# S5 stage of a two-layer decoder trunk: rows go to chunks without norm, scales are applied to the copies behind

## The chip, the cores and the metric

The kernel runs on one core of a Trainium2 chip. The metric is device time in microseconds of one execution; the time shown is the median of three runs. A profiled execution of the same kernel gives the trace.

## The reference

Two layers on x (256 tokens by 1024 features, float32). Each layer is half a SwiGLU FFN, a mixer, and half a SwiGLU FFN, each with an RMS norm ahead and added to x. The mixer of layer 0 is windowed attention and pooling; that of layer 1 is an S5 state-space layer with GELU and a gated projection:

```
def _rmsnorm(x, g):
    y = xf * lax.rsqrt(jnp.mean(xf * xf, axis=-1, keepdims=True) + EPS)
    return y * g
...
x = x + 0.5 * _swiglu(_rmsnorm(x, ffn_norm[layer, 0]), w_gate, w_up, w_down)
h = _rmsnorm(x, mix_norm[layer])
mixed = _even_mixer(h, ...) if layer % 2 == 0 else _odd_mixer(h, ...)
x = x + mixed
x = x + 0.5 * _swiglu(_rmsnorm(x, ffn_norm[layer, 1]), ...)
...
# _odd_mixer: u = h in 64 groups of 16 channels, 64 complex states a group
bu = einsum('bsgc,gpc->bsgp', u, bb)              # bb from b, a, dt
h_t = lbar * h_(t-1) + bu_t                       # over 256 tokens
y = Re(einsum('bsgp,gcp->bsgc', h, c)) + d_skip * u
z = gelu(y);  val, gate = split(z @ w_glu, 2);  mixed = val * sigmoid(gate)
```

## The kernel before

All float32 weights are split into a high part (an activation on ScalarE, `hi_of`, line 176) and a low part (a subtraction on VectorE into `wl`, line 133), and each product is three matmuls on TensorE, `mm3`. The stages follow one another: FFN f0, the even mixer, FFN f1, FFN f2, the S5 front, the gated projection (units y), FFN f3. An FFN is 11 groups of 256 hidden features; a group needs three units of weights (two of gate and up together, one of down), and a unit is loaded in two raw tiles of 512 KB (line 234).

The program is a list of steps, `S(fn, *units)`. Before each step `pump` splits as many coming units as the ring of four split units has room for, and `fill` issues their loads into four raw buffers. The list `units` is in the order of first use, but `early` puts the S5 units K0, K1, y0, y4, W0, W1 ahead at the place of the first of them. A scheduler turns the list into a queue for each engine by order of emission; a `prio(CHAIN)` moves an instruction ahead. `keep("name", i)` remembers an instruction and `behind("name")` says that what is issued under it stands behind that instruction in the order of its queue. `strict` holds TensorE to the order of emission. `hold` and `release` stop and resume the splits.

The S5 matrices are built from the parameters by the generator `s5_build`, which runs beside the steps of f1 and f2: at each paced step, of which there are five a group, `run_gens` gives it 0.8 of a turn, a turn being the code up to its next `yield`; what is left is let out at `drain`, ahead of group 8 of f2. Its first turn, in f1, issues the loads of a, log_dt, b and c (lines 741 to 756) on SP's queue. Its results go to DRAM, the matrices `dW` (input) and `dK` (the direct part within a chunk of eight tokens), and come back as the units W0, W1, K0 and K1. K takes a slot of the ring with no split, and has two loads of 1 MB (line 271). A gain vector, `gvec`, is loaded for every norm (line 320), behind the last weight load emitted.

In the tail of f2 (`tail`) the two halves c of the features of each tile t of 128 tokens are finished in turn: `x_update`, then its squares, then `norm(t, "m1", True)` (line 350 and on: squares on ScalarE with a running sum, rstd by a power on GpSimd at line 364, product with gvec on VectorE at line 142). `s5_put` (line 1010) sends the normed rows in 16 transfers of 64 KB into `V`, where a partition holds a chunk of eight tokens. `warm` has TensorE run matmuls on zeros meanwhile. Then, for each quarter k of the groups: `s5_front` (lines 1032 and 1034) copies the quarter from V into the order that the transposes want, `s5_uT` transposes, `s5_win` multiplies with the input matrices, `s5_direct` with K, `s5_scan` transposes back and runs the scan on VectorE. After the first win the order is the list `ORDER`, "f1 u1 hold d0 s0 f2 u2 w1 s1 f3 u3 ...", f for front, u for uT, w for win, d for direct, s for scan.

Of the kernel before, what the change touches and what calls it, by code (L numbers as in the profile page):

```python
# [23 lines left out]
EPS = 1e-6  # L24
# [4 lines left out]
WARM = 32  # L29
# [22 lines left out]

C_ID = 0
# [5 lines left out]
C_N = C_IF + 8  # L59


def shape_constants():
# [17 lines left out]
    c[:, C_IF:C_IF + 8] = np.asarray(INV_FREQ, np.float32)  # L80
    return c
# [23 lines left out]
def trunk_kernel(ctx: ExitStack, tc: tile.TileContext, I, out):  # L105
# [115 lines left out]
    def emit_dma(i):  # L221
# [3 lines left out]
        if kind == "W":  # L225
            r = wraw.tile([128, 1024], F32, tag="raw", name="rawW")
            c0 = (i % 2) * 1024
            with behind("put"):
                SP.dma_start(out=r, in_=s5["dW"][2 + units[i // 2][1]][:, c0:c0 + 1024])
            raws[i] = r  # L230
            return
# [18 lines left out]
    late = None  # L250

    def split_late():

        nonlocal late
        late = []

    def split_now(n, *names):
        nonlocal late
        with behind(*names):
            for _ in range(min(n, len(late))):  # L260
                keep("late", tt(*late.pop(0)))
        if not late:
            late = None

    def emit_split(i):
        if units[i][0] == "K":
            n = units[i][1]
            tl = [wsp.tile([128, 2048], F32, tag=tg, name=f"K{n}") for tg in ("wh", "wl")]
            def load(q):
                c0 = 4096 * n + 2048 * q  # L270
                SP.dma_start(out=tl[q], in_=s5["dK"][:, c0:c0 + 2048])
            load(0)
            if n:
                s5["more"] = lambda: load(1)
            else:
                load(1)
# [10 lines left out]
        for p in range(2):  # L287
# [3 lines left out]
            with behind(*(["split"] if i + p else ["norm"])):  # L291
                hi = hi_of(h[s], r)
                if late is None:
                    keep("splits", hi, tt(l[s], r, h[s].bitcast(F32), ALU.subtract))
                else:
                    keep("latehi", hi)
                    late.append((l[s], r, h[s].bitcast(F32), ALU.subtract))
# [437 lines left out]
    def s5_build():  # L735
        b = tc.alloc_tile_pool(name="s5b", bufs=1)

        def new(nm, shape, dt=F32):
            return b.tile([128] + list(shape), dt, name="b_" + nm)
        araw = b.tile([32, 2, 128], F32, name="b_araw")  # L740
        SP.dma_start(out=araw[:, 0], in_=I["s5_a_re"][0].rearrange("(j g) p -> j (g p)", g=2))
        SP.dma_start(out=araw[:, 1], in_=I["s5_a_im"][0].rearrange("(j g) p -> j (g p)", g=2))
        ld = new("ld", [64])
        SP.dma_start(out=ld, in_=I["s5_log_dt"][0].partition_broadcast(128))
        br = new("br", [2, 32, 16])
        SP.dma_start(out=br[:, 0], in_=I["s5_b_re"][0].rearrange("(j g) p c -> (g p) j c", g=2))
        SP.dma_start(out=br[:, 1], in_=I["s5_b_im"][0].rearrange("(j g) p c -> (g p) j c", g=2))
        E = s5["E"]
        cr = E[:, 1].rearrange("p a b n -> p (a b n)")[:, 0:1024].rearrange("p (r q g n) -> p r q g n", r=2, q=4, g=2)
        for r, nm in enumerate(("s5_c_re", "s5_c_im")):  # L750
            for q in range(4):
                src = I[nm][0][16 * q:16 * (q + 1)].rearrange("(j g) c p -> g j c p", g=2)
                for g in range(2):
                    SP.dma_start(out=cr[:, r, q, g], in_=src[g])
# [110 lines left out]

        X = s5["X"]
# [13 lines left out]
        st = new("st", [1024])  # L880
# [51 lines left out]
        db = cbd.rearrange("p r j g c -> p (r j g c)")[:, 0:1024]  # L932
        SP.dma_start(out=db[96:128], in_=I["s5_d"][0].partition_broadcast(32))
        Kf = K0.rearrange("p h j q n -> p (h j) (q n)")
        dv = db[96:128].rearrange("p (n c) -> p n c", c=16)
        tt(dv, dv, im[96:128].unsqueeze(1).to_broadcast([32, 64, 16]), ALU.mult)
# [49 lines left out]
    def s5_run_open():  # L986
# [4 lines left out]
        s5["G"] = p.tile([128, 2, 8, 4, 33], F32, name="G")  # L991
        R = s5["R"].rearrange("p k (q n) -> p (k q) n", n=33)
# [5 lines left out]
    def s5_put(t):  # L998

        V = s5["V"]  # L1000
        jobs = [(t, h, j) for h in range(2) for j in range(4)]
        if t == 0:
            s5["put"], jobs = jobs[-2:], jobs[:-2]
        else:
            jobs[4:4] = s5.pop("put")
        for t, h, j in jobs:
# [538 lines left out]
```

## Time and profile before

| | us |
|---|---|
| median of three runs | 956.82 |
| the three runs | 955.5 to 957.04 |
| the profiled execution | 954.66 |
| its span, first to last instruction | 952.9 |
| TensorE busy in the span | 928.8 |
| VectorE busy | 644.7 |
| ScalarE busy | 435.7 |

Times in the trace are microseconds from the start of the span. PE is TensorE's matmuls and PEld its weight loads, which overlap them; DVE is VectorE, ACT ScalarE, POOL GpSimd, and SPq the queue of SyncE, which issues most transfers; its duration is that of the issue. `out<-in` names the tiles. Of an instruction the bracket shows how long its engine was idle before it, and what ended the wait.

### The profile page before, as it was taken

Reading aid. Unit: us, or ns where it says so; the run is one execution under the profiler, and the core shown is the slowest. Engines: PE = TensorE matmul, PEld = TensorE weight load, DVE = VectorE, ACT = ScalarE, POOL = GpSimd, SP = SyncE. Lnnn points to the kernel's source line nnn. Section 1 sums busy time; section 2 is a strip of 40 time slices with the busy share of each in tenths; the row PEclk is TensorE's granted clock in tenths of the full one; section 3 lists DMA queues with packets and bytes.
Section 4 is the critical chain, followed back from the end, with each engine's and each line's share of the span. In section 5 each row is a group of like instructions: output and inputs, shape, how many; then the busy total and the mean of one; then the engine's idle time right before and its main releaser. Section 6 shows DMA issues by size and latency. Waiting matters only on the chain.

```text
span 952.9 us, 13635 instructions
## 1 busy us (share of the span) xinstructions
PE 928.8 (97%) x5208; PEld 772.4 (81%) x5208; DVE 644.7 (68%) x1097; ACT 435.7 (46%) x643; POOL 58.8 (6%) x105
## 2 busy tenths in 40 slices
PE   8999999999998999999999999999979999999998
PEld 5788888889986888888788888888659988888886
DVE  5646654488876799998675899953596575554452
ACT  6544444455635444445454444443535364444440
POOL 0000000013020000004100250000000000000000
PEclk9999999999999999999999999999999999999999
DMA  8867656644477664569756695567656457556641
GB/s 248 266 192 228 196 180 197 191 141 157 139 166 223 195 196 135 179 211 337 256 171 192 160 285 189 177 200 265 208 214 204 151 160 233 182 178 198 196 135 45
DMA packets 146033, 185.23 MB, mean 194 GB/s; under 512 B 18896, under 2 KB 128400, under 8 KB 145200
## 3 DMA queue, kind: packets, MB, share of 16 engines
q1 hardware_dynamic: 142720, 175.97, 58.9%
q0 software_dynamic: 3248, 8.39, 3.3%
q8 instruction: 41, 0.67, 0.3%
q14 instruction: 24, 0.20, 0.1%
HBM read 173.85 MB, written 9.44 MB: 192 GB/s over the span
## 4 chain that ended last, share of the span: by engine, by line
PE 72%; DVE 15%; DMA 5%; issue 3%; ACT 3%; POOL 1%; SPq 1%; POOLq 0%; ACTq 0%; DVEq 0%
PE wk L95 44%; PE acc L95 21%; PE sk L95 6%; DVE wl L133 4%; DMA raw<-in_ffn_w_up_dram 3%; DVE X L133 1%; ACT wh L176 1%; DMA raw<-in_ffn_w_down_dram 1%; POOL r L604 1%; DVE b_q L133 1%; DVE h L142 1%; DVE b_t L133 1%; DMA gvec<-in_ffn_norm_dram 1%; DVE hTl L133 1%; DVE rot L133 1%
## 5 line engine op out<-in xcount | busy, mean ns | idle before, releaser
L133 DVE TENSOR_TENSOR wl<-raw,wh 128x1024 fp32r<-128x1024 f32 x304 | 363.9, 1220 | 161.8 <-ACT wh L176 160.9
L176 ACT ACTIVATE wh<-raw 128x1024 fp32r<-128x1024 f32 x304 | 312.0, 1055 | 257.8 <-PE wk L95 98.8
L95 PE MATMUL wk<-wh,hTh 128*128 128x512 f32 (+1 forms) x868 | 230.8, 376 | 1.3 <-DVE pr L133 0.9
L95 PE MATMUL wk<-wh,hTl 128*128 128x512 f32 (+1 forms) x868 | 224.9, 370 | 1.2 <-DVE hTl L133 1.2
L95 PE MATMUL wk<-wl,hTh 128*128 128x512 f32 (+1 forms) x868 | 225.7, 370 | 0.0
L95 PEld LDWEIGHTS wk<-wh,hTl 128*128 128x128 f32 x868 | 158.5, 189 | 29.0 <-DVE hTl L133 1.6
L95 PEld LDWEIGHTS wk<-wl,hTh 128*128 128x128 f32 x868 | 158.9, 190 | 28.0 <-DVE wl L133 0.2
L95 PEld LDWEIGHTS wk<-wh,hTh 128*128 128x128 f32 x868 | 154.8, 189 | 26.5 <-DVE pr L133 1.2
L95 PE MATMUL acc<-wh,hh 128*128 128x512 f32 x352 | 141.2, 401 | 0.0
L95 PE MATMUL acc<-wh,hl 128*128 128x512 f32 x352 | 137.9, 392 | 0.5 <-DVE hl L133 0.5
L95 PE MATMUL acc<-wl,hh 128*128 128x512 f32 x352 | 137.5, 391 | 0.0
L420 ACT ACTIVATE sg<-wk 128x256 f32<-128x256 f32 x88 | 33.2, 382 | 114.8 <-PE wk L95 112.4
L133 DVE TENSOR_TENSOR pr<-sg,wk 128x256 f32<-128x256 f32 x88 | 36.6, 416 | 65.9 <-ACT sg L420 65.7
L95 PEld LDWEIGHTS acc<-wh,hl 128*128 128x128 f32 x352 | 66.0, 188 | 15.0 <-DVE hl L133 1.2
L95 PEld LDWEIGHTS acc<-wl,hh 128*128 128x128 f32 x352 | 66.3, 188 | 12.4
L95 PEld LDWEIGHTS acc<-wh,hh 128*128 128x128 f32 x352 | 66.1, 188 | 12.4 <-issue 0.2
L176 ACT ACTIVATE hh<-sk 128x256 fp32r<-128x256 f32 x88 | 32.8, 373 | 29.0 <-PE sk L95 28.9
L133 DVE TENSOR_TENSOR hl<-sk,hh 128x256 fp32r<-128x256 f32 x88 | 36.6, 418 | 5.4 <-ACT hh L176 5.3
L95 PEld LDWEIGHTS sk<-ident,pr 128*128 128x128 f32 x176 | 24.3, 140 | 12.2 <-DVE pr L133 0.6
L95 PE MATMUL sk<-ident,pr 128*128 128x128 f32 x176 | 33.6, 272 | 0.3 <-DVE pr L133 0.2
L364 POOL TENSOR_TENSOR rstd<-ss,mhalf 128x1 f32<-128x1 f32 x12 | 7.5, 623 | 389.3 <-DVE ss L142 389.3
L142 DVE SCALAR_TENSOR_TENSOR h<-x,rstd,gvec 128x512 f32<-128x512 f32 (+1 forms) x25 | 17.2, 728 | 14.9 <-DMA gvec<-in_ffn_norm_dram 7.9
(277 smaller groups left out, 679.5 us busy)
## 6 DMA issues: line engine op xcount, KB each, us to landing
raw<-in_ffn_w_gate_dram SPq DMA_DIRECT2D x88, 512.0 KB
raw<-in_ffn_w_up_dram SPq DMA_DIRECT2D x88, 512.0 KB
raw<-in_ffn_w_down_dram SPq DMA_DIRECT2D x88, 512.0 KB
raw<-in_ev_w_in_dram SPq DMA_DIRECT2D x16, 512.0 KB
raw<-in_s_w_glu_dram SPq DMA_DIRECT2D x16, 512.0 KB
raw<-in_ev_w_out_dram SPq DMA_DIRECT2D x8, 512.0 KB
K<-dK SPq DMA_DIRECT2D x4, 1024.0 KB
dK<-E POOLq DMA_DIRECT2D x36, 64.0 KB, 4.8
```

The source lines that it names most:

```text
L95: i = f(*a, **k)
L133: return DVE.tensor_tensor(out=o, in0=a, in1=b, op=op)
L142: return DVE.scalar_tensor_tensor(out=o, in0=a, scalar=s, in1=b, op0=op0, op1=op1)
L176: return ACT.activation(out=o, in_=i, func=AF.Copy)
L364: POOL.tensor_tensor(out=rstd, in0=ss[:, 2:3], in1=mhalf, op=ALU.pow)
L420: ACT.activation(out=sg, in_=ps[:, 0], func=AF.Silu)
L604: POOL.tensor_tensor(out=r8, in0=s8, in1=mhalf.to_broadcast([128, 8]), op=ALU.pow)
```

## The change

- The puts go out from x itself, right behind each `x_update` of a half c: two for each tile after c=0, six after c=1. The norm of the S5 input and its gain load are gone. The gain is multiplied into the B matrices (`gb`) and into D (`dg`) in the build.
- rstd of each row is brought into V's order, where a partition is a chunk and a column one of its eight tokens, by `s5_scale`: m8 × rstd, a small matmul with the 0/1 matrix `sel`, and a copy into `rV`. `s5_front` multiplies with it: quarters 0 and 1 by two multiplies on VectorE each, quarters 2 and 3 by eight activations on ScalarE each, with a column of rV as scale.
- `early` becomes y0, y4, W0, W1, K0, K1. K's loads are issued behind the last put emitted; the late splits (`split_late`, `split_now`, `s5["more"]`) are gone, and W's loads no longer stand behind the puts.
- The build's loads stand behind the last weight load emitted and are spread over turns, so that the generator has 12 turns more, one of them for the multiplies with gb.
- The warm matmuls are 10 + 10 instead of 32, with the small matmul of the scale between.

```diff
-WARM = 32
+WARM = 20
...
+    tok = np.arange(128)[:, None]
+    c[:, C_SE:C_SE + 64] = tok // 8 == np.arange(64)[None, :] % 16
+    c[:, C_M8:C_M8 + 8] = tok % 8 == np.arange(8)[None, :]
...
-            with behind("put"):
-                SP.dma_start(out=r, in_=s5["dW"][2 + units[i // 2][1]][:, c0:c0 + 1024])
+            SP.dma_start(out=r, in_=s5["dW"][2 + units[i // 2][1]][:, c0:c0 + 1024])
...
-            def load(q):
+            for q in range(2):
                 c0 = 4096 * n + 2048 * q
-                SP.dma_start(out=tl[q], in_=s5["dK"][:, c0:c0 + 2048])
-            load(0)
-            if n:
-                s5["more"] = lambda: load(1)
-            else:
-                load(1)
+                with behind("put"):
+                    SP.dma_start(out=tl[q], in_=s5["dK"][:, c0:c0 + 2048])
             held[units[i]] = tl
...
+        def load(o, i):
+            with behind("load"):
+                SP.dma_start(out=o, in_=i)
         araw = b.tile([32, 2, 128], F32, name="b_araw")
-        SP.dma_start(out=araw[:, 0], in_=I["s5_a_re"][0].rearrange("(j g) p -> j (g p)", g=2))
-        SP.dma_start(out=araw[:, 1], in_=I["s5_a_im"][0].rearrange("(j g) p -> j (g p)", g=2))
+        load(araw[:, 0], I["s5_a_re"][0].rearrange("(j g) p -> j (g p)", g=2))
+        load(araw[:, 1], I["s5_a_im"][0].rearrange("(j g) p -> j (g p)", g=2))
         ld = new("ld", [64])
-        SP.dma_start(out=ld, in_=I["s5_log_dt"][0].partition_broadcast(128))
+        load(ld, I["s5_log_dt"][0].partition_broadcast(128))
+        yield
         br = new("br", [2, 32, 16])
-        SP.dma_start(out=br[:, 0], in_=I["s5_b_re"][0].rearrange("(j g) p c -> (g p) j c", g=2))
-        SP.dma_start(out=br[:, 1], in_=I["s5_b_im"][0].rearrange("(j g) p c -> (g p) j c", g=2))
+        for r, nm in enumerate(("s5_b_re", "s5_b_im")):
+            load(br[:, r], I[nm][0].rearrange("(j g) p c -> (g p) j c", g=2))
+            yield
         E = s5["E"]
         cr = E[:, 1].rearrange("p a b n -> p (a b n)")[:, 0:1024].rearrange("p (r q g n) -> p r q g n", r=2, q=4, g=2)
         for r, nm in enumerate(("s5_c_re", "s5_c_im")):
             for q in range(4):
                 src = I[nm][0][16 * q:16 * (q + 1)].rearrange("(j g) c p -> g j c p", g=2)
                 for g in range(2):
-                    SP.dma_start(out=cr[:, r, q, g], in_=src[g])
+                    load(cr[:, r, q, g], src[g])
+                yield
+        st = new("st", [1024])
+        gb = st[:, 0:512].rearrange("p (j c) -> p j c", c=16)
+        for g in range(2):
+            load(gb[64 * g:64 * g + 64], I["mix_norm"][1].rearrange("(j g c) -> g j c", g=2, c=16)[g].partition_broadcast(64))
...
+        for r in range(2):
+            tt(bb[:, r], bb[:, r], gb, ALU.mult)
+        yield
...
+        dg = cbd.rearrange("p r j g c -> p (r j g c)")[96:128, 1024:2048]
         SP.dma_start(out=db[96:128], in_=I["s5_d"][0].partition_broadcast(32))
+        SP.dma_start(out=dg, in_=I["mix_norm"][1].partition_broadcast(32))
...
+        tt(db[96:128], db[96:128], dg, ALU.mult)
...
+        c = p.tile([128, 72], F32, name="sel")
+        SP.dma_start(out=c, in_=cst[:, C_SE:C_SE + 72])
+        s5["sel"], s5["m8"] = c[:, 0:64], c[:, 64:72]
+        s5["by"] = p.tile([128, 8], F32, name="by")
+        s5["rV"] = p.tile([128, 8], F32, name="rV")
...
-    def s5_put(t):
+    def s5_put(t, c):
 
         V = s5["V"]
-        jobs = [(t, h, j) for h in range(2) for j in range(4)]
-        if t == 0:
-            s5["put"], jobs = jobs[-2:], jobs[:-2]
-        else:
-            jobs[4:4] = s5.pop("put")
-        for t, h, j in jobs:
+        jobs = [(0, j) for j in (2 * c, 2 * c + 1)] + [(1, j) for j in range(4 * c)]
+        for h, j in jobs:
             r = slice(64 * t + 16 * j, 64 * t + 16 * j + 16)
             c0 = 256 * j + 128 * h
             with prio(CHAIN), behind("put"):
-                keep("put", SP.dma_start(out=V[r, h].rearrange("p t q g c -> p t (q g c)"), in_=hn[t][:, c0:c0 + 128]))
+                keep("put", SP.dma_start(out=V[r, h].rearrange("p t q g c -> p t (q g c)"), in_=xs[t][:, c0:c0 + 128]))
+
+    def s5_scale(t, after):
+
+        ss = sums.pop(t)
+        rstd = tmp.tile([128, 1], F32, tag="rstd", name="rstd")
+        sel, m8, by, rV = s5["sel"], s5["m8"], s5["by"], s5["rV"]
+        o = slice(64 * t, 64 * t + 64)
+        with prio(CHAIN):
+            stt(ss[:, 2:3], ss[:, 0:1], EPS, ss[:, 1:2], ALU.add, ALU.add)
+            POOL.tensor_tensor(out=rstd, in0=ss[:, 2:3], in1=mhalf, op=ALU.pow)
+            ts(by, m8, rstd, ALU.mult)
+            ps = sk((128, 8))
+            with behind(after):
+                keep("scale", mm(ps[o], sel, by, True, True))
+            DVE.tensor_copy(out=rV[o], in_=ps[o])
 
     def warm(n, w):
 
         ps = wk((128, 4, 128))
         for _ in range(n):
-            mm(ps, w, w.unsqueeze(1).to_broadcast([128, 4, 128]), True, True)
+            keep("warm", mm(ps, w, w.unsqueeze(1).to_broadcast([128, 4, 128]), True, True))
...
-        with prio(CHAIN), behind("latehi", "late" if k == 0 else "U0" if k == 1 else f"Sb{k - 2}"):
-            for g in range(2):
-                o, i = V2[:, q, g], V[:, h, :, q, g].rearrange("p t q c -> p q t c")
-                if g or k:
-                    ACT.copy(out=o, in_=i)
-                else:
-                    DVE.tensor_copy(out=o, in_=i)
+        with prio(CHAIN), behind(*(["U0v"] if k == 1 else [f"Sb{k - 2}", f"U{k - 1}"])):
+            if k < 2:
+                for g in range(2):
+                    tt(V2[:, q, g], V[:, h, :, q, g].rearrange("p t q c -> p q t c"),
+                       s5["rV"].unsqueeze(1).unsqueeze(3).to_broadcast([128, 2, 8, 16]), ALU.mult)
+                return
+            for tau in range(8):
+                ACT.activation(out=V2[:, q, :, tau], in_=V[:, h, tau, q], func=AF.Copy, scale=s5["rV"][:, tau:tau + 1])
...
-                    ACT.copy(out=U[:, 2 * k:2 * k + 2, :, :, 16 * t:16 * t + 16].rearrange("p q g j n -> p (q g) j n"),
-                             in_=ps[:, :, :, t].rearrange("p q g j n -> p (q g) j n"))
+                    keep(f"U{k}", ACT.copy(
+                        out=U[:, 2 * k:2 * k + 2, :, :, 16 * t:16 * t + 16].rearrange("p q g j n -> p (q g) j n"),
+                        in_=ps[:, :, :, t].rearrange("p q g j n -> p (q g) j n")))
...
+        each(0, 0)
...
-    S(lambda: load_g("m1", I["mix_norm"][1]))
-
-    def put(t):
-        def f():
-            S(lambda: norm(t, "m1", True))
-            S(lambda: s5_put(t))
-        return f
     S(s5_early)
-    tail(2, put(0), lambda: None)
+    tail(2, lambda: None, lambda: None, lambda t, c: S(lambda: s5_put(t, c)))
 
     def warm_s5():
         s5["zero"] = w = tmp.tile([128, 128], mybir.dt.bfloat16, tag="warm", name="warm")
         POOL.memset(w, 0.0)
         with behind("down"):
-            warm(WARM, w)
+            warm(WARM // 2, w)
+        s5_scale(0, "down")
+        s5_scale(1, "warm")
+        with behind("scale"):
+            warm(WARM // 2, w)
             for k in range(2):
                 clear(k)
         table(AF.Gelu_apprx_tanh)
     S(warm_s5)
-    put(1)()
-
-    def ahead():
-        release("square")
-        split_late()
-        pump()
-        split_now(3, "norm")
-        s5["more"]()
-    S(ahead)
+    S(lambda: release("square"))
...
-    early = [("K", 0), ("K", 1), ("y", 0), ("y", 4), ("W", 0), ("W", 1)]
+    early = [("y", 0), ("y", 4), ("W", 0), ("W", 1), ("K", 0), ("K", 1)]
```

## Rows read from the trace of the kernel before

**Rows 1.** The page, busy time of each engine, share of the span, instructions.

```profile
PE 928.8 (97%) x5208; PEld 772.4 (81%) x5208; DVE 644.7 (68%) x1097; ACT 435.7 (46%) x643; POOL 58.8 (6%) x105
```

**Rows 2.** Windows; columns: stretch, length, busy of PE, PEld, DVE, ACT, POOL, PE clock, DMA, GB/s.

```profile
300.00:676.00 376.00, 375.21 (x1817) 307.72 (x1816) 295.41 (x561) 167.56 (x239) 38.23 (x73) 1.00 0.67 213
...
542.00:616.00 74.00, 74.00 (x336) 61.03 (x335) 70.79 (x118) 32.65 (x44) 18.01 (x35) 1.00 0.74 220
...
625.00:671.00 46.00, 46.00 (x210) 37.87 (x209) 19.23 (x25) 16.21 (x24) 0.00 (x0) 1.00 0.73 251
...
661.00:674.45 13.45, 13.45 (x63) 11.05 (x62) 3.45 (x8) 2.98 (x8) 0.57 (x1) 1.00 1.02 417
```

**Rows 3.** The chain that ended last; columns: start, us, what.

```profile
284.40 5.38 DMA gvec<-in_ffn_norm_dram
```

**Rows 4.** Timeline of SP's queue, 262 to 330 us; columns: start, us, instruction.

```profile
271.89 8.22 SPq L747 DMA_DIRECT2D b_br<-in_s_b_im_dram  x1
...
283.51 0.84 SPq L234 DMA_DIRECT2D raw<-in_ffn_w_gate_dram  x1
...
284.40 0.50 SPq L320 DMA_DIRECT2D gvec<-in_ffn_norm_dram  x1
```

**Rows 5.** Timeline of all engines, 262 to 304 us.

```profile
274.38 2.35 DVE L133 TENSOR_TENSOR wl<-raw,wh 128x1024 fp32r<-128x1024 f32 x2
```

**Rows 6.** Timeline of all engines, 283 to 296 us; idle before and its releaser in brackets.

```profile
285.77 0.56 POOL L364 TENSOR_TENSOR rstd<-ss,mhalf 128x1 f32<-128x1 f32 x1 [10.45 <-DVE ss L142]
...
288.19 1.06 ACT L176 ACTIVATE wh<-raw 128x1024 fp32r<-128x1024 f32 x1 [2.70 <-DMA raw<-in_ffn_w_gate_dram]
...
289.88 1.42 DVE L142 SCALAR_TENSOR_TENSOR h<-x,rstd,gvec 128x512 f32<-128x512 f32 x2 [4.20 <-DMA gvec<-in_ffn_norm_dram]
...
290.78 0.30 PE L95 MATMUL sk<-ident,h 128*128 128x128 f32 x1 [3.60 <-DVE h L142]
```

**Rows 7.** Windows, the stretch behind the gap at f1's head.

```profile
290.00:295.00 5.00, 3.86 (x14) 3.27 (x14) 4.32 (x6) 2.75 (x5) 0.00 (x0) 0.66 0.97 290
```

**Rows 8.** Timeline of all engines, 655 to 692 us, the S5 opening.

```profile
659.52 1.24 SPq L271 DMA_DIRECT2D K<-dK  x2
...
677.09 7.08 PE L95 MATMUL wk<-warm 128*128 128x512 bf16 x32
...
677.28 0.69 DVE L142 SCALAR_TENSOR_TENSOR x<-acc,x 128x512 f32<-128x512 f32 x1 [0.67 <-PE acc L95]
...
679.65 1.54 DVE L142 SCALAR_TENSOR_TENSOR h<-x,rstd,gvec 128x256 f32<-128x256 f32 x3 [0.73 <-POOL rstd L364]
...
685.01 0.40 ACT L1032 COPY h<-V 128x256 f32<-128x256 f32 x1 [0.98 <-ACT wh L176]
...
685.44 0.41 PE L95 MATMUL wk<-ident,h 128*128 128x128 f32 x2 [0.84 <-ACT h L1032]
...
688.01 1.08 PE L95 MATMUL acc<-K,U 128*32 128x128 f32 x32
...
689.03 0.66 PE L95 MATMUL sk<-ident,Sb 128*128 128x128 f32 x4
...
689.78 1.29 DVE L133 TENSOR_TENSOR h<-sk,E 128x512 f32<-128x512 f32 x2 [2.33 <-ACT h L1032]
```

**Rows 9.** Timeline of DVE, 372 to 378 us.

```profile
372.70 1.22 DVE L133 TENSOR_TENSOR wl<-raw,wh 128x1024 fp32r<-128x1024 f32 x1
...
373.84 0.69 DVE L133 TENSOR_TENSOR X<-X,b_q 128x512 f32<-128x512 f32 x1
```

**Rows 10.** The line of the puts: duration min/median/max in ns, first and last start.

```profile
L1010 SPq DMA_DIRECT2D V<-h x16: 547/597/689, 675.1 to 685.9; - x16
```

**Rows 11.** The chain that ended last, 660 to 700 us: from issue to landing.

```profile
675.79 2.40 DMA V<-h
```

**Rows 12.** Groups of ACT by form: busy us, mean ns of one, idle before.

```profile
L647 ACT ACTIVATE sc<-sc,mx 128x128 f32<-128x128 f32 x8 | 2.5, 389 | 1.7 <-DVE mx L137 1.7
...
L357 ACT ACTIVATE pre<-x 128x1 f32<-128x1 f32 x3 | 0.6, 203 | 0.0
```

More of the change, by code (lines that the diff above doesn't have):

```diff
@@ L58 @@
 C_IF = C_IM + 16
-C_N = C_IF + 8
+C_SE = C_IF + 8
+C_M8 = C_SE + 64
+C_N = C_M8 + 8
 def shape_constants():
@@ L248, in fill @@
             state["dma"] += 1
[L250 to L263, printed above, removed]
     def emit_split(i):
@@ L292, in emit_split @@
                 hi = hi_of(h[s], r)
-                if late is None:
-                    keep("splits", hi, tt(l[s], r, h[s].bitcast(F32), ALU.subtract))
-                else:
-                    keep("latehi", hi)
-                    late.append((l[s], r, h[s].bitcast(F32), ALU.subtract))
+                keep("splits", hi, tt(l[s], r, h[s].bitcast(F32), ALU.subtract))
         held[units[i]] = (h, l)
@@ L878, in s5_build @@
             yield
-        st = new("st", [1024])
         turned = [x.rearrange("p (k r j i) -> p k r j i", k=2, r=2, j=4)
@@ L1027, in s5_front @@
         V, V2 = s5["V"], hn[h].rearrange("p (q g t c) -> p q g t c", q=4, g=2, t=8)
-        with prio(CHAIN), behind("latehi", "late" if k == 0 else "U0" if k == 1 else f"Sb{k - 2}"):
-            for g in range(2):
-                o, i = V2[:, q, g], V[:, h, :, q, g].rearrange("p t q c -> p q t c")
-                if g or k:
-                    ACT.copy(out=o, in_=i)
-                else:
-                    DVE.tensor_copy(out=o, in_=i)
+        with prio(CHAIN), behind(*(["U0v"] if k == 1 else [f"Sb{k - 2}", f"U{k - 1}"])):
[6 more added lines that the diff above has]
+                ACT.activation(out=V2[:, q, :, tau], in_=V[:, h, tau, q], func=AF.Copy, scale=s5["rV"][:, tau:tau + 1])
     def s5_uT(k):
@@ L1251, in ffn_joint, with tail @@
                     HID(f, g, t)
-    def tail(f, fin_a, fin_b):
+    def tail(f, fin_a, fin_b, each=lambda t, c: None):
         S(strict(f == 1))
@@ L1260, in tail @@
         S(lambda: x_update(0, 0.5, (0,)))
+        each(0, 0)
         dn(f, NG - 1, 0, (1,))
         S(lambda: x_update(0, 0.5, (1,)))
+        each(0, 1)
         fin_a()
@@ L1270, in tail @@
         S(lambda: x_update(1, 0.5, (0,)))
+        each(1, 0)
         fin_b()
@@ L1273, in tail @@
         S(lambda: x_update(1, 0.5, (1,)))
+        each(1, 1)
     def hold():
@@ L1438, in trunk_kernel @@
     S(lambda: s5_uT(0))
-    S(lambda: split_now(1, "U0v"))
     S(lambda: s5_win(0))
```

## The prediction, made before the change was run

> **What bounds the kernel now.** I read the page first: TensorE is busy 97% of the span, VectorE 68% [rows 1]. So an edit pays only where TensorE stands idle, or runs below full clock, or where it makes such a place. The chain of waits between 230 and 330 us gives one place that the change touches, the head of f1; the timeline from 655 to 692 us gives the other, the opening of the S5 stage. Between them, from 300 to 676 us, TensorE is busy for 375.2 of 376 us [rows 2]: nothing can be gained there, only lost.
>
> At the head of f1 the chain passes through SP's issue of a weight tile and through 5.38 us of the transfer of the gain vector gvec [rows 3]. SP's queue says why so late: the load of b_im alone holds SP for 8.22 us, c_re follows, and only at 283.51 the next weight tile and at 284.40 gvec are issued [rows 4]. The tile's buffer had been free since its last reader, the second of two subtractions that take 2.35 us from 274.38, so since 276.7 at the latest [rows 5]. The norm had its rstd at 286.33 (285.77 + 0.56), waited 4.20 us for gvec and started at 289.88; TensorE waited 3.60 us for the first normed half, from 287.2 to 290.78 [rows 6]. Behind that gap the granted clock is 0.66 in the mean of 290 to 295 us, so part of that stretch ran at 1.2 GHz [rows 7].
>
> In the S5 opening the last update of x is at 677.28, the norm at 679.65 in three pieces, then the puts; the first copy of the chunks starts at 685.01, d0 runs at 688.01, the transposes of s0 at 689.03, and the first VectorE operation of the scan at 689.78 [rows 8]. From there VectorE sets the pace for some 23 us, so what moves 689.78 moves the end.
>
> **The change part by part.**
>
> *A. Build loads behind the weight loads, spread over the steps.* SP no longer stands in them before gvec. gvec goes out right behind its weight tile at about 277 instead of 284.40; with the same 5.38 us it lands at about 282.5, ahead of rstd. The norm then starts at 286.4 instead of 289.9: −3.5 us, and nothing else is late next, because TensorE's last product ends at 287.2 and the first half of the norm (1.42 us for two) is done at 287.1. The low clock: of the 5 us window 3.86 us are busy at 0.66; at 1.00 this is 3.86 × 0.34 = 1.3 us less. I take 1.5 (the whole window gives 1.7). Sum −5.0; bounds −3.5 (the low clock comes anyway) and −5.9 (all of the 4.20 us wait and 1.7).
>
> The loads themselves now stand between weight tiles in groups 1 to 3 of f1. The two loads of the gain gb are 64-byte pieces, 2,048 each, half of those of b_im, so by its row [rows 4] they hold SP 4.1 us each. A weight tile waits up to 8.2 us then; the weights are loaded four raw tiles ahead and split up to three units ahead. f1 and f2 are 22 groups between 287.2 and 677.3, 17.7 us a group and 5.9 us a unit, so the cover is 12 to 18 us: cost 0. If the cover is gone the cost is the 8.2 us. The Trainium skill (DMA: Bandwidth & Descriptors, "Why small descriptors are slow (HBM only)") gives a fixed overhead of some 3 cycles a packet, two beats of data for a 64-byte piece, by which the two loads would take (my estimate from it) about 1.5 us together and no stall would be possible: the something else below, 0.06, would be 0.03. The trace's 8.22 us for the same kind of load disagrees with it, and the measurement decides.
>
> *B. One more multiply and 12 more steps of the build generator.* The generator is called 0.8 times a paced step, five paced steps a group: 12 / 0.8 = 15 steps = 3 groups = 53 us later. VectorE work of the build that now lies in 542 to 616 us (70.79 us busy of 74) slides towards the end of f2, where 19.23 of 46 us are busy [rows 2]. Its own part there is 70.79 − 74 × 19.23/46 = 39.9 us. It would start near 596 and has 75 us until 671, where the last updates of x begin; the ordinary work of that stretch is 31.4 us, the splits of y0 and y4 moved there are four subtractions, 4.7 us. Together 76 us of 75: full, but just done. The splits of f2 keep going through it: each step of the build waits for the one before, and in the full stretch at 372 us they alternate with wl one by one [rows 9]. I take 0; bounds 0 and +10 (rival 3).
>
> *C. Puts without norm, scales behind.* The puts of h=0 start when x is updated (677.28 + 0.69 = 677.97) instead of behind the norm. Two puts at 0.597 us each on SP [rows 10] and the landing of 2.40 us [rows 11] give all chunks at 681.6. rstd is ready at 679.6; one multiply, one small matmul and one copy give rV by about 680.5, hidden. The two multiplies of the first front, at the 0.40 of a copy of the same size [rows 8], end at 682.4, and the 20 filler matmuls (0.22 each, in two halves round the small matmul, then the clears) end at about 683. First transposes 683.0 instead of 685.44: 2.4 us earlier, if nothing else is late.
>
> *D. K loads behind the puts.* Something is: K0. Before, it was issued at 659 and long on chip. Now SP issues it behind the last of six puts, 677.97 + 6 × 0.6 = 681.6, first half away at 682.2. A put of 64 KB lands 2.40 us after its issue [rows 11]; at 417 GB/s, the most that the queues moved [rows 2], 0.2 us of it is data, so 2.2 us is fixed. K0 has 2.10 MB: 5.0 us. It lands at 682.2 + 2.2 + 5.0 = 689.4. K1 comes behind it in the same queue; the weight tile issued at 283.51 is read at 288.19, gvec behind it only at 289.88 [rows 4, 6], so I take transfers in order. d0 stands ahead of s0 in TensorE's strict order: from its start to s0's transposes 1.02 us, to the scan another 0.75 [rows 8]. The scan starts at 691.2 instead of 689.78: +1.4. TensorE is idle some 3.5 us for K0, as long as the gap before the low clock of rows 7. If the clock falls again, d0 and s0 take up to 1.2 us more; I take 0.5. Sum +1.9, bounds +0.9 (landing half a microsecond earlier, no clock loss) and +3.1 (half a microsecond later, 1.2).
>
> *E. Front 2 and 3 as eight scaled activations each.* Nothing before does this; the nearest rows are a one-element activation, 0.203 us, and one of 128x128 with a bias from memory, 0.389 us [rows 12]. So 1.6 to 3.1 us against 0.7 for two copies; 128x64 lies between, I take 2.0. Hidden in the forecast, since u2 stands behind d0's wait for K0; if that wait is gone (rival 1) it costs at most 3.1 − 0.7 = 2.4 us, which would take back what rival 1 gains over none of C.
>
> *F. y0 and y4 split ahead.* They take ring slots earlier, hidden under f2's end; y1 and y5 then wait for those slots in the projection. Cost 0.
>
> **Sum.** −5.0 + 1.9 = −3.1 us. The profiled execution takes 954.66 us, 2.2 below the median 956.82; the differences are put on the median: 953.7. Its own range from the bounds: −5.9 + 0.9 = −5.0 (951.8) to −3.5 + 3.1 = −0.4 (956.4). A measurement here tells about 0.2%, 1.9 us, from no change.
>
> **Rivals.**
> 1. K0 isn't late (the loads go out before the puts, or land sooner than 686.5). Then the 2.4 us of C are kept: −5.0 − 2.4 = −7.4, 949.4. For it: every microsecond by which SP is free sooner counts. Against: 2.1 MB needs 5.0 us at the highest rate seen.
> 2. The gain of A isn't had: gvec is still late, for instance because its pin to the last weight load puts it behind one whose buffer frees late. Then +1.9 alone, 958.7. Against: the buffer's last reader was done at 276.7.
> 3. Slower: the build's VectorE work is let out in one block at the drain before group 8 of f2, ahead of the splits emitted later. Place: VectorE, from about 621 us. Twelve calls of three operations at 0.6 us (70.79 us / 118 in rows 2) are a block of 21.6 us; above the cover of 12 to 18 us TensorE stands, 3.6 to 9.8, say 7. It decides from a block of 15 to 21 us on. −3.1 + 7 = +3.9, 960.7. For it: 76 of 75 us. Against: rows 9.
>
> **Chances.** Forecast 0.48, rival 1 0.17, rival 2 0.17, rival 3 0.12, something else 0.06 (half of it the stall behind the gain's loads). Faster by over 0.2% (below 954.9): three quarters of the forecast, rival 1, and half of the rest, 0.36 + 0.17 + 0.03 = 0.56. Within: a quarter of the forecast and half of rival 2, 0.12 + 0.09 = 0.21. Slower: 0.23, what is left. Range 948.8 to 959.2: from just under rival 1 to just over rival 2, leaving out rival 3 and some of the rest.
>
> **What would show it.** In the trace after: gvec issued before 280 and no TensorE gap over 1 us at 287 (A); first transposes of S5 5.7 us behind the start of the last x update instead of 8.2 (C); d0 waiting for the transfer of K some 3 us, and a scan that starts 13.9 us behind that update instead of 12.5 (D); no wait for wl between 600 and 671 (B). Wrong: a low clock at a new place, or a TensorE gap in f1's groups 1 to 3 behind the small loads.

## The result, and the profile of the changed kernel

The changed kernel takes 961.31 us in the median of eight runs (959.16 to 964.76), the kernel before 956.17 in the runs beside them: ratio 1.0053, interval 1.0040 to 1.0066. It is slower by some 5 us, where 953.7 was forecast and 948.8 to 959.2 was the range.

The profiled execution took 963.66 us, with a span of 961.9; that of before was a quick one (954.66, span 952.9), so the two traces differ by 9.0 us and the medians by 5.1. The span can be cut at five instructions that all kernels have: rstd for the norm at f1's head, rstd at f2's head, the start of the last update of x in f2, the first VectorE operation of the scan, and the first subtraction into hTl behind the scan. Each column is the time in us from the instruction of the column ahead to its own; a difference in a column says where a kernel won or lost.

| kernel | rstd f1 to rstd f2 | to last update of x | to the scan | scan | to the end |
|---|---|---|---|---|---|
| before | 193.79 | 197.72 | 12.50 | 20.74 | 242.38 |
| changed | 191.23 | 200.24 | 21.45 | 20.74 | 242.14 |
| x1_spread_alone | 190.77 | 199.09 | 22.15 | 20.73 | 242.93 |
| x2_k0_ahead | 191.17 | 199.17 | 10.04 | 25.02 | 242.25 |
| x3_k0_before_w | 189.85 | 198.21 | 16.69 | 20.81 | 242.18 |
| x4_gain_early | 189.39 | 198.10 | 21.20 | 21.59 | 242.19 |
| x5_no_spread | 197.84 | 198.10 | 19.69 | 20.85 | 242.16 |
| x6_zero_late | 195.98 | 198.15 | 21.17 | 20.86 | 242.21 |
| y2_k0_ahead_k1_gain | 189.92 | 198.31 | 10.25 | 21.86 | 242.20 |
| y3_fronts_dve | 188.71 | 198.10 | 10.04 | 23.07 | 242.15 |
| z1_loads_as_before | 193.37 | 198.19 | 20.55 | 20.73 | 242.18 |
| z2_changed_again | 189.52 | 200.19 | 21.62 | 21.69 | 242.23 |

So in this trace the changed kernel won 2.6 us up to f2's head, lost 2.5 in f2, and lost 9.0 between the last update of x and the scan. That last stretch is the result. In the second execution that was profiled (z2_changed_again) the three are 4.3 won, 2.5 lost and 9.1 lost, so the first of them is not steady.

**f1's head.** The timeline of SP's queue of the changed kernel, where [rows 4] stood:

```profile
275.89 0.37 SPq L239 DMA_DIRECT2D raw<-in_ffn_w_gate_dram  x1
276.60 2.07 SPq L302 DMA_DIRECT2D gvec<-in_ffn_norm_dram  x1
```

The timeline of all engines, where [rows 6] stood:

```profile
286.10 0.56 POOL L346 TENSOR_TENSOR rstd<-ss,mhalf 128x1 f32<-128x1 f32 x1 [9.59 <-DVE ss L148]
...
288.02 1.06 ACT L182 ACTIVATE wh<-raw 128x1024 fp32r<-128x1024 f32 x1 [2.20 <-DMA raw<-in_ffn_w_gate_dram]
...
289.36 1.41 DVE L148 SCALAR_TENSOR_TENSOR h<-x,rstd,gvec 128x512 f32<-128x512 f32 x2 [3.34 <-DMA gvec<-in_ffn_norm_dram]
...
290.25 0.30 PE L101 MATMUL sk<-ident,h 128*128 128x128 f32 x1 [1.84 <-DVE h L148]
```

gvec goes out at 276.60, as forecast and 7.8 us sooner than before, and yet the norm waits for it until 289.36: 12.7 us from issue instead of 5.4. The weight tile issued at 275.89 is read at 288.02, 12.1 us later, where it was 4.7 before. What runs beside them stands in GpSimd's timeline, and the windows show the transfer engines full (the last two columns are their share and GB/s, the one ahead the clock):

```profile
271.69 4.82 POOL L754 DMA_DIRECT2D dK<-b_zero  x7 [0.37 <-POOL b_zero L751]
```

```profile
275.00:280.00 5.00, 5.00 (x24) 4.14 (x23) 2.00 (x2) 1.57 (x3) 1.51 (x3) 1.00 1.00 204
280.00:285.00 5.00, 5.00 (x24) 4.14 (x23) 3.68 (x4) 1.72 (x4) 0.00 (x0) 1.00 0.94 229
285.00:290.00 5.00, 3.41 (x16) 2.48 (x14) 0.87 (x3) 1.78 (x3) 0.56 (x1) 1.00 1.01 337
290.00:295.00 5.00, 4.38 (x23) 3.68 (x24) 5.00 (x8) 3.35 (x7) 0.00 (x0) 1.00 0.41 143
```

The gap of TensorE is 1.84 us instead of 3.60, and the clock stays at 1.00 from 290 to 295 us, where it was 0.66 [rows 7]. In z2_changed_again gvec is used 11.1 us after its issue and TensorE waits 0.7 us in all for the norm at this head, where it waits 2.6 here.

**f2's head.** A new wait, which before had not; timeline of all engines:

```profile
477.33 0.56 POOL L346 TENSOR_TENSOR rstd<-ss,mhalf 128x1 f32<-128x1 f32 x1 [5.74 <-DVE ss L148]
...
480.07 1.41 DVE L148 SCALAR_TENSOR_TENSOR h<-x,rstd,gvec 128x512 f32<-128x512 f32 x2 [2.89 <-DMA gvec<-in_ffn_norm_dram]
...
480.97 1.29 PE L101 MATMUL sk<-ident,h 128*128 128x128 f32 x8 [1.39 <-DVE h L148]
```

The build's writes of dW, which the 12 more turns moved here, end just ahead of it (GpSimd's timeline):

```profile
465.59 2.18 POOL L890 DMA_DIRECT2D dW<-b_st  x4 [169.37 <-DVE b_st L885]
469.49 2.11 POOL L890 DMA_DIRECT2D dW<-E  x4 [1.73 <-DVE E L885]
```

**The S5 opening.** SP's queue and then all engines, where [rows 8] stood:

```profile
666.50 0.32 SPq L234 DMA_DIRECT2D rawW<-dW  x1
672.15 10.31 SPq L1009 DMA_DIRECT2D V<-x  x16
682.63 1.42 SPq L234 DMA_DIRECT2D rawW<-dW  x3
684.40 2.09 SPq L262 DMA_DIRECT2D K<-dK  x4
```

```profile
667.45 2.36 DVE L139 TENSOR_TENSOR wl<-raw,wh 128x1024 fp32r<-128x1024 f32 x2 [0.53 <-ACT wh L182]
...
677.57 0.69 DVE L148 SCALAR_TENSOR_TENSOR x<-acc,x 128x512 f32<-128x512 f32 x1 [0.67 <-PE acc L101]
...
683.10 0.38 PE L101 MATMUL wk<-ident,h 128*128 128x128 f32 x2
...
686.23 2.02 ACT L1049 ACTIVATE h<-V,rV 128x64 f32<-128x64 f32 x8
...
693.53 0.64 PE L101 MATMUL acc<-K,U 128*32 128x128 f32 x4 [7.87 <-DMA K<-dK]
...
696.01 1.92 PE L101 MATMUL acc<-K,U 128*32 128x128 f32 x28 [1.83 <-DMA K<-dK]
...
697.86 1.12 PE L101 MATMUL sk<-ident,Sb 128*128 128x128 f32 x4
...
699.02 1.29 DVE L139 TENSOR_TENSOR h<-sk,E 128x512 f32<-128x512 f32 x2 [14.40 <-PE sk L101]
```

The front is as forecast: the first transposes start 5.5 us behind the last update of x (5.7 forecast, 8.2 before). Then TensorE waits 9.7 us for K0 and VectorE 14.4 us for the scan. Three loads of W stand between the last put and K0. Their buffers had been free: the last two subtractions that read the raw tiles of y0 and y4 end at 669.81, 2.3 us ahead of the first put at 672.15, and SP issues nothing between 666.82 and that put. It is their place in the queue that puts them behind. While TensorE waits, its clock goes to 1.2 GHz and stays there for the rest of d0 and for s0 (windows; the clock is the third value from the end):

```profile
690.00:694.00 4.00, 0.47 (x4) 0.19 (x4) 0.00 (x0) 0.00 (x0) 0.00 (x0) 0.50 1.01 421
694.00:698.00 4.00, 2.17 (x31) 1.50 (x30) 0.00 (x0) 0.00 (x0) 0.00 (x0) 0.50 1.00 424
```

28 matmuls of d0 take 1.92 us there, where all 32 took 1.08 before, and s0's four transposes 1.12 instead of 0.66 [rows 8].

### The profile page after: what moved, and what is told of

Its sections match the earlier page's. It is cut to its first block, busy times and chain, and to the rows that moved or that the text cites. A ratio compares the mean times of both kernels' runs of the same rounds, so it can differ in the third digit from the quotient of the medians.

```text
span 961.9 us, 13640 instructions
## 1 busy us (share of the span) xinstructions
PE 929.3 (97%) x5200; PEld 772.6 (80%) x5200; DVE 645.1 (67%) x1102; ACT 437.8 (46%) x652; POOL 58.3 (6%) x105
## 4 chain that ended last, share of the span: by engine, by line
PE 83%; DVE 8%; DMA 5%; ACT 1%; issue 1%; POOL 1%; SPq 1%; POOLq 0%; DVEq 0%; ACTq 0%
PE wk L101 52%; PE acc L101 25%; PE sk L101 6%; DMA gvec<-in_ffn_norm_dram 3%; DVE wl L139 2%; DMA K<-dK 1%; DVE h L148 1%; DVE hTl L139 1%; POOL r L586 1%; DVE rot L139 1%; DVE G L1136 1%; DVE h L139 1%; DMA raw<-in_ffn_w_down_dram 0%; DVE G L139 0%; DVE qk L139 0%
## 5 line engine op out<-in xcount | busy, mean ns | idle before, releaser
L182 ACT ACTIVATE hTh<-sk 128x512 fp32r<-128x512 f32 x24 | 15.9, 689 | 22.4 <-PE sk L101 22.0
```

Of the source, the lines that this page charges most:

```text
L182: return ACT.activation(out=o, in_=i, func=AF.Copy)
```

## The experiments

**x1_spread_alone** is the kernel before with part A alone. Edit:

```diff
-        SP.dma_start(out=br[:, 0], in_=...)
-        SP.dma_start(out=br[:, 1], in_=...)
+        for r, nm in enumerate(("s5_b_re", "s5_b_im")):
+            load(br[:, r], ...)          # load: behind("load")
+            yield
...
+                yield                    # and so for a, log_dt and c
```

> The kernel before with part A alone: the build's loads behind the weight loads and spread over 11 more turns. Theory (transfers): gvec of f1 is issued some 8 us sooner but lands at about 289, beside the zero fill of dK; some 2 us are won by 460 us, and the writes of dW, which slide to the head of f2, take them back there by a late gvec of f2. So the time stays within 1 us of before's 956.2. Rival (the prediction's term A): 5.0 us faster, 951.2.

Measured 961.31, ratio 1.0045 (1.0028 to 1.0061). Both expectations missed. The FFNs went as the theory had it: 3.0 us won up to f2's head, 1.4 lost in f2. But the S5 opening, which this kernel has unchanged, took 22.15 us instead of 12.50. SP's queue, ScalarE's timeline and TensorE's waits say why:

```profile
672.56 11.58 SPq L1016 DMA_DIRECT2D V<-h  x16
684.19 1.14 SPq L234 DMA_DIRECT2D raw<-in_s_w_glu_dram  x2
```

```profile
688.04 1.06 ACT L176 ACTIVATE wh<-raw 128x1024 fp32r<-128x1024 f32 x1 [8.39 <-DMA raw<-in_s_w_glu_dram]
```

```profile
PE wk L95 <- DVE h L1040: 8.6, 1, 8.6
```

With the build later, the loads of y4 come behind the puts in SP's queue (before, all four loads of y0 and y4 were ahead of them); the late high parts wait for them, and the copies of the first front stand behind those. Here too the buffers were free long before: the subtractions that read them end at 657.6 and 659.3, the first put goes out at 672.56. Why the scheduler places these loads behind the puts isn't shown. So the later build has a cost in the opening, with the old order of units as with the new one.

**x2_k0_ahead** is the changed kernel with K0 loaded first:

```diff
-    early = [("y", 0), ("y", 4), ("W", 0), ("W", 1), ("K", 0), ("K", 1)]
+    early = [("K", 0), ("y", 0), ("y", 4), ("W", 0), ("W", 1), ("K", 1)]
```

> The changed kernel with K0 as the first of the early units, so that it is loaded at about 660 us and y4 is split behind the end of f2 instead. Theory (the loss is K0 behind the puts and behind three loads of W): no wait of d0 for K, the scan starts at about 687.5 instead of 699.0, TensorE keeps its clock; some 11 us faster than the changed kernel, 950.3, so faster than before. Rival (the late split of y4 takes its place on VectorE and ScalarE ahead of the first front): scan at 690 or later, 953 or more. Second rival (puts without norm and scales cost something of their own): no faster than before, 956 or more.

Measured 954.63, ratio 0.9976 (0.9961 to 0.9991): faster than before, though not by what was expected. The opening is better than forecast (timeline of all engines):

```profile
675.39 0.69 DVE L148 SCALAR_TENSOR_TENSOR x<-acc,x 128x512 f32<-128x512 f32 x1 [0.67 <-PE acc L101]
...
683.73 1.08 PE L101 MATMUL acc<-K,U 128*32 128x128 f32 x32
685.43 1.29 DVE L139 TENSOR_TENSOR h<-sk,E 128x512 f32<-128x512 f32 x2 [2.69 <-PE sk L101]
...
698.44 0.41 PE L101 MATMUL acc<-K,U 128*32 128x128 f32 x4 [0.76 <-DMA K<-dK]
700.96 1.92 PE L101 MATMUL acc<-K,U 128*32 128x128 f32 x28 [2.10 <-DMA K<-dK]
```

10.04 us from the last update of x to the scan, 2.5 less than before and 11.4 less than in the changed kernel. The wait came back one step on, at d2, for K1, which now stood behind four loads of W; the scan stage took 25.02 us instead of 20.74.

**x3_k0_before_w** is the changed kernel with W behind K0 in the queue:

```diff
+    early = [("y", 0), ("y", 4), ("K", 0), ("W", 0), ("W", 1), ("K", 1)]
...
+            if units[state["dma"] // 2][0] == "W" and ("K", 0) not in held:
+                break
```

> The changed kernel with K0 emitted ahead of W, so that the loads of W stand behind K0's on the queue. Theory (transfers in the order of the queue, 417 GB/s): three loads of 0.52 MB less ahead of K0 are 3.8 us, so K0 lands at about 692 instead of 696, and the scan starts at 695; 957.5. Rival (K0's transfer is bounded by its own size and the puts, not by W): the scan starts no more than 1.4 us sooner, the issue time of three loads; 960.

Measured 955.39, ratio 0.9983 (0.9971 to 0.9995), 2 us better than expected; the two FFNs were 3.4 us quicker in this trace than in the first one of the changed kernel, which the edit doesn't explain. Timeline of all engines:

```profile
673.22 0.69 DVE L148 SCALAR_TENSOR_TENSOR x<-acc,x 128x512 f32<-128x512 f32 x1 [0.67 <-PE acc L101]
678.51 0.81 SPq L264 DMA_DIRECT2D K<-dK  x2
...
684.42 0.41 PE L101 MATMUL acc<-K,U 128*32 128x128 f32 x4 [3.10 <-DMA K<-dK]
686.91 1.92 PE L101 MATMUL acc<-K,U 128*32 128x128 f32 x28 [2.07 <-DMA K<-dK]
...
689.91 1.29 DVE L139 TENSOR_TENSOR h<-sk,E 128x512 f32<-128x512 f32 x2 [9.65 <-PE sk L101]
```

From the last update of x to the scan 16.69 us instead of 21.45: the loads of W ahead of K0 are 4.8 us, 3.8 of them expected as data. Nothing stands between the puts and K0 here, as the prediction had assumed, and the clock still falls.

**x4_gain_early** is the changed kernel with the gains of f1 and f2 loaded sooner (issued at 254.0 and 428.5 us):

```diff
-    p510 m1 t00 ... o21 o31 l o30        # l: load of f1's gvec
+    ... p400 l x00 ...
...
-    ffn_joint(1, 1, NG)
+    ffn_joint(1, 1, 8)
     S(lambda: load_g("f2", I["ffn_norm"][1, 0]))
+    ffn_joint(1, 8, NG)
```

> The changed kernel with the gain vectors of f1 and f2 loaded a good deal sooner. Theory (the two late gvec are what is left of the gap at f1's head and what makes the new gap at f2's head): no wait of TensorE for the norm at 288 and 480; at f1's head the split of the first gate tile, landed at 288.0, then sets the start, so 1.2 us there and 1.4 us at f2's head: 2.6 us faster than the changed kernel, 958.7. Rival (the weights at both heads are as late as gvec): under 1 us.

Measured 958.91, ratio 1.0024 (1.0014 to 1.0033): as expected. VectorE's timeline at the two heads, where the norm now waits for rstd alone:

```profile
284.83 1.41 DVE L148 SCALAR_TENSOR_TENSOR h<-x,rstd,gvec 128x512 f32<-128x512 f32 x2 [0.69 <-POOL rstd L346]
...
474.21 1.42 DVE L148 SCALAR_TENSOR_TENSOR h<-x,rstd,gvec 128x512 f32<-128x512 f32 x2 [0.75 <-POOL rstd L346]
```

Against before, 4.0 us are won from f1's rstd to the last update of x (193.79 + 197.72 against 189.39 + 198.10). Against the second profile of the changed kernel (z2_changed_again) 2.2 us are won, 2.1 of them in f2's column; so the gain at f2's head is steady, and the one expected at f1's head depends on which execution is compared.

**x5_no_spread** is the changed kernel without the turns that spread the loads:

```diff
         load(ld, ...)
-        yield
...
             load(br[:, r], ...)
-            yield
...
                 load(cr[:, r, q, g], src[g])
-                yield
```

> The changed kernel with its build loads behind the weight loads, but without the 11 turns that spread them: the build runs some 48 us sooner than in the changed kernel. Theory (the delay of the build is a cost of its own: dW's writes fall on the head of f2, and VectorE's full stretch falls on the end of f2, so that raw buffers come free late and three loads of W go behind the puts): gvec of f2 is on time, which gives back 2.2 us, and one load of W less ahead of K gives 1.3: 957.8. Rival (the delay is harmless, the burst of loads costs): 961 or more, with a gap of TensorE in groups 1 to 3 of f1.

Measured 965.20, ratio 1.0094 (1.0072 to 1.0116). The rival holds for f1: the burst holds SP from 307 to 327 us, and a weight tile behind it is late (SP's queue, and the two largest of TensorE's waits from 300 to 480 us):

```profile
307.76 6.02 SPq L724 DMA_DIRECT2D b_br<-in_s_b_im_dram  x1
...
325.75 1.99 SPq L724 DMA_DIRECT2D b_st<-in_mix_norm_dram  x2
327.84 1.24 SPq L239 DMA_DIRECT2D raw<-in_ffn_w_down_dram  x1
```

```profile
PE sk L101 <- DVE pr L139: 3.3, 2, 3.0
PE acc L101 <- ACT wh L182: 1.4, 1, 1.4
```

From f1's rstd to f2's it takes 6.6 us more than the changed kernel's first profile. The wait of 1.4 us, at 332 to 334 us, stands directly behind that tile. The one of 3.0 us ends at 356.8 and is for VectorE, which is 94% busy from 350 to 360 us with splits and with the build; how much of it the burst makes isn't shown, because without the turns the build's work comes sooner too. In the changed kernel TensorE has neither wait, so the 11 turns keep both hidden. The other half of the theory holds as to its size: f2 costs 198.10 instead of 200.24 (the norm still waits 1.27 us for gvec, TensorE doesn't), and with two loads of W behind the puts instead of three the opening is 1.8 us shorter.

**x6_zero_late** is the changed kernel with the zero fill of dK made to wait for dt:

```diff
-        POOL.memset(zero, 0.0)
-        for tau in range(7): POOL.dma_start(out=dK[...], in_=zero[...])
...
+        with behind("dt"):
+            DVE.memset(zero, 0.0)
+        for tau in range(7): POOL.dma_start(out=dK[...], in_=zero[...])
```

> The changed kernel with the zero fill of dK (seven transfers from GpSimd's queue, at 271 us) made to wait for dt, so that it runs later in f1. Theory (the zero fill shares the transfer engines with gvec and the first weights of f1): gvec, issued at about 276, lands at 283 or sooner instead of 289, TensorE doesn't wait for it at f1's head, and 2.5 us are won: 958.8. Rival (gvec is slow by itself or by the weight tiles beside it): it lands at 287 or later and the time stays at 961.

Measured 966.49, ratio 1.0109 (1.0082 to 1.0136). At f1's head the theory holds as to the cause: gvec, issued at 274.6, is there before rstd, and TensorE waits 0.4 us for the norm instead of 2.6 (0.7 in z2_changed_again). But the fill then runs at 319.7 us beside the spread loads. SP takes 8.42 us to issue two loads of c_re there, 3.71 in the changed kernel; a weight tile behind them is late, TensorE waits 4.4 us, and the granted clock is 0.50 from 336 to 340 us (VectorE's timeline, GpSimd's, TensorE's waits from 300 to 480):

```profile
284.72 1.42 DVE L148 SCALAR_TENSOR_TENSOR h<-x,rstd,gvec 128x512 f32<-128x512 f32 x2 [0.67 <-POOL rstd L346]
```

```profile
319.74 4.83 POOL L791 DMA_DIRECT2D dK<-b_zero  x7 [28.01 <-ACT hh L182]
```

```profile
PE sk L101 <- DVE pr L139: 4.4, 1, 4.4
```

So the fill delays gvec in the one place and weights in the other.

**z1_loads_as_before** is the changed kernel with part A undone (the loads of x5_no_spread without `behind("load")`).

> The changed kernel with part A undone: the build's loads are issued in its first turn ahead of f1's weights and without more turns, as before (the two loads of the gain gb with them). Theory (part A is worth some 2 to 3 us in the changed kernel, as far as gvec and dW let it, and the loss lies in K): f1's head as before, 19.7 us from the last update of x to the scan as in x5_no_spread, 7.2 us slower than before: 963.8. Rival (the delay of the build by part A made the loss in the opening): the opening takes some 14 us as forecast, 958.5.

Measured 963.73, ratio 1.0074 (1.0057 to 1.0091), as expected: f1's head as before, the opening 20.55 us. Part A is worth some 2 us inside the changed kernel (ratios of 1.0074 and 1.0053 to before, whose intervals overlap), and all but 0.9 us of the loss in the opening is there without it.

**z2_changed_again** is the changed kernel once more.

> The changed kernel once more, for a second profile. Theory (the time varies with the landing of gvec at the heads of f1 and f2 and of K, by 2 to 3 us in all): the last update of x between 674 and 678 us, from there 20 to 22 us to the scan. Rival (the first profile was an outlier in the opening): under 18 us there.

One run of 961.75 us, span 960.0. The opening took 21.62 us; from f1's rstd to f2's 189.52 instead of 191.23. The loss in the opening is steady, the gain at f1's head varies with the landing of gvec: the norm waits for it 1.65 us here and 3.34 in the first profile.

**y2_k0_ahead_k1_gain** puts the three findings together: x2_k0_ahead, x4_gain_early, and K1 ahead of W1:

```diff
+    early = [("K", 0), ("y", 0), ("y", 4), ("W", 0), ("K", 1), ("W", 1)]
...
+            if units[state["dma"] // 2] == ("W", 1) and ("K", 1) not in held:
+                break
```

> The changed kernel with K0 ahead of y0, the gain vectors of f1 and f2 loaded sooner, and K1 emitted between W0 and W1. Theory (the three causes found add up): last update of x 5.6 us sooner than before, 10.0 us from there to the scan instead of 12.5, no wait for K1: 8 us faster than before, 949. Rival (they share a cause, or a new wait takes the place): not below x2_k0_ahead, 954.6.

Measured 949.50, ratio 0.9929 (0.9909 to 0.9950): faster than both kernels, and no wait for K1. Not all of the theory came true: up to the last update of x 3.3 us are won over before in the traces, not 5.6, and the scan stage is 1.1 us longer, with a split of y4 (1.22 us, at 687.95) inside it. VectorE's timeline, the last update of x and the scan:

```profile
673.69 0.69 DVE L148 SCALAR_TENSOR_TENSOR x<-acc,x 128x512 f32<-128x512 f32 x1 [0.67 <-PE acc L101]
...
683.94 1.29 DVE L139 TENSOR_TENSOR h<-sk,E 128x512 f32<-128x512 f32 x2 [2.69 <-PE sk L101]
```

**y3_fronts_dve** is y2 with fronts 2 and 3 as multiplies on VectorE ahead of the scan:

```diff
-    f1 u1 hold d0 s0 f2 u2 w1 s1 f3 u3
+    f1 f2 f3 u1 hold d0 s0 u2 w1 s1 u3
...
-            if k < 2:
+            if True:
```

> The kernel y2_k0_ahead_k1_gain with fronts 2 and 3 on VectorE as well, in its idle 2.7 us ahead of the scan, instead of eight activations each on ScalarE. Theory (the eight activations of 2.0 us stand in TensorE's path to s1 and s2, but VectorE's scan hides all but a part): up to 1 us faster than y2, 948. Rival (VectorE is late for the scan by four multiplies): 1 us slower than y2.

Measured 950.74, ratio 0.9941 (0.9925 to 0.9957): no faster than y2. The scan starts no later (10.04 us), but the scan stage is 1.2 us longer. VectorE's timeline shows where the multiplies went:

```profile
682.98 0.69 DVE L139 TENSOR_TENSOR h<-sk,E 128x512 f32<-128x512 f32 x1 [2.69 <-PE sk L101]
683.59 1.42 DVE L139 TENSOR_TENSOR h<-V,rV 128x256 f32<-128x256 f32 x4
```

VectorE stood idle for 2.69 us ahead of the scan, and the four multiplies ran behind the scan's first operation, where their 1.42 us lengthen it. So this run doesn't show what fronts 2 and 3 would cost in the idle stretch.

## Why the prediction was wrong, step by step

**D is the step that failed.** It had the mechanism, K0 behind the puts and d0 ahead of s0, and put the opening, with C's gain in it, at 1.9 us more. It measured 9.0 (21.45 against 12.50). Between the two traces the whole change is 9.0 us longer where 3.1 less were forecast, a miss of 12.1: 7.1 are D, and 5.0 are A and B, which together won nothing instead of 5.0. The second profile of the changed kernel gives 7.2 and 3.2. The difference of 7.1 by D's own terms:

- "Now SP issues it behind the last of six puts": it is issued behind three loads of W as well. Of the 21.45 us, 4.8 go with them when K0 is put ahead (x3_k0_before_w). That is the cause that was left out: the change takes W's loads from behind the puts in the program, and the prediction gave them no place in the queue; three of the four still came behind the puts, with their buffers free, and in x5_no_spread and z1_loads_as_before two.
- In x3_k0_before_w K0 is issued 5.3 us behind the last update of x (4.3 forecast) and its second half is used 8.4 us later (7.8 forecast): +1.0 and +0.6. The 2.2 us fixed and 5.0 us of data were nearly right.
- d0's rest and s0 take 3.0 us at the low clock (686.91 to 689.91), where 1.77 was the term at full clock and 0.5 was allowed for the clock: +0.7. The upper bound, 1.2 us for the clock, is what it cost.

4.8 + 1.0 + 0.6 + 0.7 = 7.1.

**A was half right.** The issue of gvec came where it was forecast, and the clock behind the gap too. Up to f2's head 2.6 us were won in the first profile and 4.3 in the second, 5.0 forecast; that the gap costs about what was said is shown by x4_gain_early too, which wins 4.0 us over before in the two FFNs. What failed is "with the same 5.38 us it lands at about 282.5": SP's queue was no longer the bound, and x6_zero_late shows what was: without the zero fill beside it gvec is in time. Rival 2 named the outcome, a late gvec, with another cause.

**B was not free.** The cost that was looked for, TensorE waiting because VectorE is full at the end of f2, did not come: the build's last operation is at 664, and TensorE doesn't wait for a split between 500 and 676 us. But two others did. dW's writes came to f2's head, where gvec then took 8.1 us to land and 2.5 us were lost; x4_gain_early shows that the late gvec is 2.1 us of that loss. That the writes of dW make it late goes with most of the traces, but no run moved them alone. Before, the last four were issued 9.1 us ahead of gvec, and the norm didn't wait for it; at 2.4 us ahead gvec was used 8.2 and 7.9 us after its issue (the two profiles of the changed kernel), at 2.6 us ahead 7.2 (x2_k0_ahead), and at 2.9 to 3.1 us ahead 6.2 to 6.6 (x3_k0_before_w, x5_no_spread, z1_loads_as_before). But in x1_spread_alone it was 7.1 with the last four 5.9 us ahead and two more behind gvec's issue, and the weight loads just ahead of gvec come closer together too in the traces where it is late. And with the 11 turns more loads came behind the puts in SP's queue: two of y4 in x1_spread_alone, one more of W in the changed kernel (21.45 us against 19.69 in x5_no_spread).

**C was right.** The first transposes came 2.6 us sooner against the last update of x (2.4 forecast), and with K0 on chip this arrives at the scan: 10.04 and 10.25 us instead of 12.50.

**E was right in size**: eight activations take 2.02 us. They were called hidden, and are in the changed kernel but for 1.3 us of TensorE's waits; with K0 on time they cost 2.3 us of waits in two places. Whether moving them wins any of that isn't shown, since in y3_fronts_dve the multiplies ran inside the scan.

**F held**: from the scan's end to the end of the kernel it takes 242.14 us, 242.38 before.

**The loads of gb** hold SP for 1.98 us together, not 8.2 (SP's queue of the changed kernel):

```profile
320.86 3.71 SPq L724 DMA_DIRECT2D b_br<-in_s_b_im_dram  x1
...
356.28 1.98 SPq L724 DMA_DIRECT2D b_st<-in_mix_norm_dram  x2
```

The row of b_im, 8.22 us, had been taken beside the zero fill. Away from it the same load holds SP 3.71 us here, and 6.02 in the burst of x5_no_spread; so the fill is a part of the 8.22, and half of a row of b_im for each load of gb would still be too much. Why isn't shown. The rule of the Trainium skill (DMA: Bandwidth & Descriptors, "Why small descriptors are slow (HBM only)"), by which the estimate was 1.5 us, was nearer to the measured 1.98 than the row. The conclusion that no stall is possible holds for these two loads in the changed kernel, where TensorE has no wait from 300 to 470 us; for the whole burst it doesn't, as x5_no_spread shows.

**Rival 1** (K0 not late) is what y2 made true. That 949.4 was its price and 949.5 the time of y2 is partly luck: the price has 5.0 us for A and 2.4 for C, and y2's trace wins 3.3 up to the last update of x and 2.3 in the opening and loses 1.1 in the scan stage; its span is 4.9 us shorter than that of before, where the medians differ by 7.1. **Rival 3** did not come.

## What to carry to other kernels

When a load is moved behind something in a queue, list everything else that is already behind it there, and count those transfers too; here the moved load cost some 6.7 us by itself (16.69 in x3_k0_before_w against 10.04 in x2_k0_ahead), and three loads of another matrix 4.8 on top. Look in the trace for loads that stand in a queue with their buffers free. When a queue is cleared, ask what the next bound of the transfer is: gvec left 8 us sooner and was used half a microsecond sooner in the first profile, because bulk writes of another queue ran beside it. Parts don't add: part A alone lost 4 us, the rest without it lost 7 (z1_loads_as_before) and the whole lost 5, while all parts with K0 and the gains loaded early and K1 ahead of W1 won 7.

## What the runs showed of the hardware

- A load of 512 KB, gvec of f1, was used 5.4 us after its issue before, and 12.7 and 11.1 us after it in the two profiles of the changed kernel. There seven zero-filling transfers from another engine's queue were issued 5 us ahead of it; with the fill moved away the norm didn't wait for it (x6_zero_late). The transfer engines were 94 to 101% busy then at 204 to 337 GB/s (275 to 290 us, first profile), while the same engines moved 421 at 1.01 during the loads of K.
- One load's issue held SP for different times: that of b_im 8.22 us beside the zero fill (before), 6.02 in the burst (x5_no_spread) and 3.71 spread out (the changed kernel); two loads of c_re 8.42 us beside the fill (x6_zero_late) and 3.71 away from it.
- TensorE's granted clock fell to 0.50, 1.2 GHz, within the 7.9 us that it stood for K0, and was still there from 694 to 698 us, while d0 ran; in the changed kernel's f1 head, after a gap of 1.84 us, it stayed at 1.00, where before it had fallen behind one of 3.60.
